# FFN down projections as seven products of half the tokens, half the K and half the columns, with x kept in DRAM

## The chip, the core and the metric

The kernel runs on one core of a Trainium2 chip. The metric is the device time of one execution in microseconds, the median over several executions.

TensorE (PE) multiplies and transposes, VectorE (DVE) and ScalarE (ACT) do elementwise work, GpSimd (POOL) and SyncE (SP) mostly issue DMAs here. ScalarE's queue also issues some DMAs, between its own instructions. Each engine runs its instructions in the order in which the built program lists them, and a waiting instruction holds up all that stand behind it on its engine.

## What is computed

Two layers of a decoder trunk on 512 tokens with D_MODEL 1024. Each layer has a mixer of four parallel branches, and then a SwiGLU feed-forward network (FFN) with residual, which is the part that matters here:

```python
FFN_DIM = ((8 * D_MODEL // 3 + 255) // 256) * 256      # 2816

def hybrid_layer(x, ...):
    ...
    x = x + merged @ w_out

    hf = rmsnorm(x, norm_ffn)
    gate, up = jnp.split(hf @ ffn_w_up, 2, axis=-1)
    return x + (jax.nn.silu(gate) * up) @ ffn_w_down
```

All inputs are float32. The down projection is a product of a 512 x 2816 matrix of activations with the 2816 x 1024 matrix `ffn_w_down[l]`, once for each of the two layers.

## The kernel before

**Three products for one.** Every float32 matrix is kept as a high part in a reduced format (`F32R`) and a low part, the rest. `mm3` (line 267) multiplies two such pairs with three matmuls: high by high, high by low, low by high. In the profile these are lines 270, 271 and 272. A matmul takes a 128x128 stationary tile and up to 512 moving columns.

**Weights.** `Chunk` (line 212) loads one block of weights from DRAM into a `w_raw` tile of 128 x 2048 floats (line 216, on SP's queue), and splits it in pieces of 128 x 1024: ScalarE rounds into `w_hi` (through the helper `A`, line 97), then VectorE subtracts into `w_lo` (line 225). There are two `w_raw` buffers (`RAW_BUFS`) and three each of `w_hi` and `w_lo` (`W_BUFS`). The splits are issued with raised priority (`AHEAD`), and the compiler's scheduler decides where they stand in each engine's order.

**Feature-major and token-major.** `features` has the weights stationary and 512 tokens moving, and its result has features on the partitions. `tokens_wide` has the activations stationary and 512 weight columns moving; its result has tokens on the partitions.

**PSUM.** There are three banks named `mm`, two named `at`, three named `tr` (transposes).

**The FFN** (`ffn`, line 1037) goes through its 2816 inner columns in two parts, of 6 and of 5 chunks of 256 columns. For each chunk it multiplies `h` by the gate and by the up weights (2 x 8 K-tiles x 2 column blocks x 3 = 96 matmuls), scales, applies silu, multiplies, and splits the result into `a_hi` and `a_lo`. After the chunks of a part comes the down projection of that part, with 12 or 10 K-tiles of 128:

- `residual` (line 1000) does it feature-major, for both parts of layer 0 and for the first part of layer 1. For each pair of 128 output columns it loads the weights (1024 KB for 8 K-tiles, then the rest), multiplies, adds the result onto the tile `xT`, which stays in SBUF through the FFN, and in layer 0's second part makes the next layer's `h` (`h_chunk`: cast, difference, square, sum of squares) and sends the chunk of x to the DRAM tensor `x_spill` for the next layer.
- In layer 1's first part, `transposed` turns each finished chunk of `xT` into the token-major `x_tok` with four transposes.
- `final` (line 1023) does layer 1's second part token-major with `tokens_wide`, adds onto `x_tok` and writes the output.

`residual` is also used for the mixer's output projection `w_out`, which reads x from `x_spill` into `xT` (line 987) and makes the FFN's `h`.

Of the kernel before, what the change touches and what calls it, by code (L numbers as in the profile page):

```python
# [69 lines left out]
def hybrid_trunk(ctx: ExitStack, tc: tile.TileContext, x, mem, positions, norm_mix, w_in, conv_w,  # L70
# [41 lines left out]
    def f(ap):  # L112
        return ap.bitcast(F32)
# [153 lines left out]
    def mm3(ps, a, b, first, last):  # L267
        ah, al = a
        bh, bl = b
        pe.matmul(ps, ah, bh, start=first, stop=False)  # L270
        pe.matmul(ps, ah, bl, start=False, stop=False)  # L271
        pe.matmul(ps, al, bh, start=False, stop=last)  # L272

    x_dram = nc.dram_tensor("x_spill", [P, KD, S], F32, kind="Internal").ap()
    kv_dram = [nc.dram_tensor(f"kv{l}", [P, 4, 2, 2, MEM], F32, kind="Internal").ap() for l in range(DEPTH)]
# [225 lines left out]
    def mixer(l, h, norms, cm, cf):  # L501
# [174 lines left out]
        with pool_("dsa") as dp:  # L676
# [46 lines left out]
            with pool_("idx") as ip:  # L723
# [120 lines left out]
                mgp = cf.enter_context(pool_("mgp", "left"))  # L844
# [139 lines left out]
        res = cf.enter_context(tc.tile_pool(name="res", bufs=1))  # L984
# [13 lines left out]
        return h2, ssq2, xT  # L998

    def residual(xT, w2d, a, kt, cols, h2, ssq2, gain, spill=False, done=None):  # L1000
        for m0 in range(0, KD, cols // P):
            ws = []
            k0 = 0
            per = 2048 // cols
            while k0 < kt:
                n = min(per, kt - k0)
                ws.append((k0, n, wchunk(w2d[k0 * P:(k0 + n) * P, m0 * P:m0 * P + cols], n, cols)))
                k0 += n
            pss = [mm_ps() for _ in range(cols // P)]
            for js in ([range(cols // P)] if m0 + cols // P < KD else [[j] for j in range(cols // P)]):  # L1010
                for k0, n, w in ws:
                    features(w, a, js, k0, kt, [pss[j] for j in js])
            for j in range(cols // P):
                m = m0 + j
                dve.tensor_add(xT[:, m, :], xT[:, m, :], pss[j])
                if h2 is not None:
                    h_chunk(h2, ssq2, m, gain(m), xT[:, m, :])
                if spill:
                    nc.scalar.dma_start(x_dram[:, m, :], xT[:, m, :])
                if done is not None:  # L1020
                    done(m)

    def final(x_tok, w2d, a, kt):
        for m0 in range(0, D, 512):
            cols = slice(m0, m0 + 512)
            ws = [wchunk(w2d[k0 * P:min(k0 + 4, kt) * P, cols], min(4, kt - k0), 512) for k0 in range(0, kt, 4)]
            pss = [mm_ps() for _ in range(MM_BUFS)] + [at_ps()]
            tokens_wide(ws, a, kt, pss)
# [87 lines left out]
```

## Time and profile before

| | |
|---|---|
| median of 3 runs | 2047.56 us (2047.41 to 2047.92) |
| the profiled execution | 2047.48 us |
| its span in the profile | 2045.4 us |
| VectorE, ScalarE busy | 62%, 50% of the span |
| granted TensorE clock, mean | 0.999 of full speed |
| moved by DMA | 203.79 MB, 100 GB/s in the mean |
| layer 0: FFN's first up stage, first down stage | from 700 us; 823.6 to 889 us |
| layer 0: second down stage | 1006 to 1060 us |
| layer 1: second down stage | 1987 to 2041 us |

The span runs from the first to the last instruction that the profile shows; the execution's own time is 2 us longer. Rows of a group name line, engine, operation, output and inputs (buffer numbers left out), how often, and times in ns; in the views of one tile they give the shortest, median and longest duration. Rows of waits say who waited for whom, the sum in us, how often and the longest. Rows of DMA issues end with the median time from issue to landing in us.

### The profile page before, as it was taken

What the parts mean: (1) busy time and instruction counts of PE and PEld (TensorE: products, weight loads), DVE (VectorE), ACT (ScalarE), POOL (GpSimd) and SP (SyncE); (2) the same over time, 40 slices, a digit from 0 to 9 for tenths busy, and PEclk for the clock granted to TensorE, in tenths of its full rate; (3) what the DMA queues carried; (4) which work ended last, traced back from release to release, by engine and by line L of the source; (5) the groups of instructions that cost most, each with busy time, mean ns of one, the idle gap of its engine ahead of it and who ended that gap; (6) DMA issues with size and microseconds to landing.
All of it is one profiled execution on the core that took longest, in us unless ns stands there. A gap on an engine that the chain in (4) does not pass through costs nothing.

```text
span 2045.4 us, 26581 instructions
## 1 busy us (share of the span) xinstructions
PE 2034.5 (99%) x10348; PEld 1715.8 (84%) x10348; DVE 1269.3 (62%) x2507; ACT 1017.5 (50%) x1834; POOL 9.8 (0%) x33
## 2 busy tenths in 40 slices
PE   8999999999999999999999999999999999999999
PEld 8998988888888888888889898888888888888887
DVE  6779998547676544334457889963777754533442
ACT  7653655766665423223355456576767633322331
POOL 0000000000000000000000000000000000000000
PEclk9999999999999999999999999999999999999999
DMA  7632232223233232233243213322223322323322
GB/s 253 220 89 94 68 93 93 64 71 93 78 118 113 83 103 93 93 105 102 87 155 94 88 58 107 97 76 63 83 83 101 126 90 96 103 75 111 97 79 93
DMA packets 187709, 203.79 MB, mean 100 GB/s; under 512 B 4270, under 2 KB 176384, under 8 KB 187456
## 3 DMA queue, kind: packets, MB, share of 16 engines
q1 hardware_dynamic: 183872, 193.56, 29.8%
q10 hardware_dynamic: 3552, 8.41, 1.1%
q8 instruction: 81, 1.33, 0.3%
q14 instruction: 44, 0.36, 0.1%
q0 software_dynamic: 160, 0.13, 0.0%
HBM read 191.60 MB, written 10.49 MB: 99 GB/s over the span
## 4 chain that ended last, share of the span: by engine, by line
PE 99%; DMA 1%; DVE 0%; ACT 0%; SPq 0%; issue 0%; DVEq 0%
PE mm L270 30%; PE mm L272 30%; PE mm L271 30%; PE tr L715 1%; PE tr L709 1%; PE at L686 1%; PE at L685 1%; PE at L272 1%; PE at L270 1%; PE at L271 1%; DMA w_raw<-in_mem_w_kv_dram 1%; PE at L963 0%; PE at L937 0%; PE tr L653 0%; PE tr L754 0%; PE tr L972 0%
## 5 line engine op out<-in xcount | busy, mean ns | idle before, releaser
L270 PE MATMUL mm<-h_hi,w_hi 128*128 128x512 f32 x1664 | 653.0, 393 | 0.0
L271 PE MATMUL mm<-h_lo,w_hi 128*128 128x512 f32 x1664 | 652.1, 392 | 0.0
L272 PE MATMUL mm<-h_hi,w_lo 128*128 128x512 f32 x1664 | 650.1, 392 | 0.0
L225 DVE TENSOR_TENSOR w_lo<-w_raw,w_hi 128x1024 fp32r<-128x1024 f32 (+1 forms) x346 | 419.5, 1213 | 364.5 <-ACT w_hi L97 361.3
L97 ACT ACTIVATE w_hi<-w_raw 128x1024 fp32r<-128x1024 f32 (+1 forms) x346 | 363.4, 1051 | 460.8 <-PE mm L271 414.5
L272 PEld LDWEIGHTS mm<-h_hi,w_lo 128*128 128x128 f32 x1664 | 312.8, 188 | 64.8 <-issue 1.2
L270 PEld LDWEIGHTS mm<-h_hi,w_hi 128*128 128x128 f32 x1664 | 312.8, 188 | 64.5 <-issue 2.2
L271 PEld LDWEIGHTS mm<-h_lo,w_hi 128*128 128x128 f32 x1664 | 312.9, 188 | 63.8 <-issue 2.0
L272 PE MATMUL mm<-w_hi,h_lo 128*128 128x256 f32 (+1 forms) x448 | 128.2, 286 | 0.0
L271 PE MATMUL mm<-w_lo,h_hi 128*128 128x256 f32 (+1 forms) x448 | 127.0, 285 | 0.0
L270 PE MATMUL mm<-w_hi,h_hi 128*128 128x256 f32 (+1 forms) x448 | 127.0, 285 | 0.0
L271 PE MATMUL mm<-a_lo,w_hi 128*128 128x512 f32 x272 | 106.3, 391 | 0.0
L270 PE MATMUL mm<-a_hi,w_hi 128*128 128x512 f32 x272 | 106.0, 390 | 0.0
L272 PE MATMUL mm<-a_hi,w_lo 128*128 128x512 f32 x272 | 105.8, 391 | 0.0
L270 PE MATMUL mm<-y_hi,w_hi 128*128 128x512 f32 x256 | 101.4, 397 | 0.0
L272 PE MATMUL mm<-y_hi,w_lo 128*128 128x512 f32 x256 | 100.6, 393 | 0.0
L271 PE MATMUL mm<-y_lo,w_hi 128*128 128x512 f32 x256 | 100.3, 392 | 0.0
L272 PEld LDWEIGHTS mm<-w_hi,h_lo 128*128 128x128 f32 x448 | 85.8, 191 | 1.4 <-issue 0.8
L270 PEld LDWEIGHTS mm<-w_hi,h_hi 128*128 128x128 f32 x448 | 85.3, 191 | 1.2 <-issue 0.8
L271 PEld LDWEIGHTS mm<-w_lo,h_hi 128*128 128x128 f32 x448 | 85.6, 191 | 0.6
L97 ACT ACTIVATE a_hi<-fg 128x512 fp32r<-128x512 f32 x44 | 27.8, 633 | 109.4 <-DVE fg L1065 109.4
L97 ACT ACTIVATE prob<-prob,small 128x128 f32<-128x128 f32 (+3 forms) x128 | 69.2, 554 | 15.2 <-DVE small L698 14.6
(358 smaller groups left out, 2946.9 us busy)
## 6 DMA issues: line engine op xcount, KB each, us to landing
w_raw<-in_w_in_dram SPq DMA_DIRECT2D x72, 1024.0 KB, 5.3
w_raw<-in_ffn_w_up_dram SPq DMA_DIRECT2D x44, 1024.0 KB, 5.1
w_raw<-in_w_lift_dram SPq DMA_DIRECT2D x32, 512.0 KB, 3.5
w_raw<-in_ffn_w_down_dram SPq DMA_DIRECT2D x16, 1024.0 KB, 5.5
w_raw<-in_mem_w_kv_dram SPq DMA_DIRECT2D x8, 1024.0 KB, 5.4
w_raw<-in_w_out_dram SPq DMA_DIRECT2D x8, 1024.0 KB, 5.2
w_raw<-in_ffn_w_down_dram SPq DMA_DIRECT2D x10, 512.0 KB, 3.4
kv<-kv ACTq DMA_DIRECT2D x8, 512.0 KB, 3.2
```

What stands on the lines that cost most here:

```text
L97: i = act.activation(dst, src, func, **kw)
L225: dve.tensor_sub(lo, raw[:, k:e], f(hi))
L270: pe.matmul(ps, ah, bh, start=first, stop=False)
L271: pe.matmul(ps, ah, bl, start=False, stop=False)
L272: pe.matmul(ps, al, bh, start=False, stop=last)
L685: pe.matmul(ps, q[:, hh, s], k[0][:, :n], start=True, stop=False)
L686: pe.matmul(ps, q[:, hh, s], k[1][:, :n], start=False, stop=True)
L709: pe.transpose(pp[:, (2 * e + i) * P:(2 * e + i + 1) * P], probs[2 * i + e][:, b * P:(b + 1) * P], ident)
L715: pe.matmul(pv[e * HD:(e + 1) * HD, :], vt[:, b, :], pt[:, b, e * 2 * P:(e + 1) * 2 * P], start=b == 0, stop=b == t)
```

## The change

The down projection of a part becomes seven products instead of eight, after the scheme of Strassen and Winograd. The activations are cut into two halves of 256 tokens and, in each chunk of 256 inner columns, into two K-tiles of 128 (a "round" is one such pair); the weights into two halves of 512 columns and the same K-tiles. Each of the seven products multiplies a sum or difference of activation blocks with a sum or difference of weight blocks, and the results are collected token-major in a tile `acc`.

- `operands` replaces the split of the activations: it makes the seven activation operands of a round (256 tokens each), high and low.
- `down` replaces `residual` and `final` for the FFN. It runs four passes over the rounds of the part, each with weight loads of its own (`raw_tile` and `split` use the same `w_raw`, `w_hi` and `w_lo` buffers as `Chunk`). Pass one has two products a round with plain weights; pass two two products whose weights are made by two subtractions on VectorE, and one of these differences is written to a new DRAM tensor `t2_spill` by ScalarE's queue; pass three two products, one with a difference; pass four one product, whose weights are a difference with what was written to `t2_spill`. Between the passes `evict` adds the PSUM banks onto `acc`.
- x is no longer held in SBUF through the FFN. The mixer's `residual` writes it to `x_spill`. Layer 1 reads it back in eight chunks during its first part and transposes them into `acc` (`x_in`). Layer 0 adds it at the end: `x_out` reads a chunk on GpSimd's queue into one of three `x_c` buffers, transposes four blocks of `acc`, adds, makes the next `h` and writes the chunk back to `x_spill`. The first four chunks are placed in pass four of the second part, the other four behind it.

```diff
-    def residual(xT, w2d, a, kt, cols, h2, ssq2, gain, spill=False, done=None):
+    def residual(xT, w2d, a, kt, cols, h2, ssq2, gain):
...
+                nc.scalar.dma_start(x_dram[:, m, :], xT[:, m, :])
...
+    def raw_tile():
+        return wpool.tile([P, 2048], F32, name="w_raw", bufs=RAW_BUFS)
+
+    def split(src):
+
+        n = src.shape[1]
+        hi, lo = (wpool.tile([P, 1024], F32R, name=nm, bufs=W_BUFS)[:, :n * 512].rearrange("p (k n) -> p k n", n=512)
+                  for nm in ("w_hi", "w_lo"))
+        with tc.high_priority(offset=AHEAD):
+            A(hi, src, AF.Copy)
+            dve.tensor_sub(lo, src, f(hi))
+        return [(hi[:, k, :], lo[:, k, :]) for k in range(n)]
+
+    def operands(fp, g0, g1):
+
+        hi, lo = (fp.tile([P, 7, HALF], F32R, name=nm, bufs=6) for nm in ("a_hi", "a_lo"))
+
+        def put(o, n, src):
+            h_, l_ = (x[:, o:o + n, :].rearrange("p a b -> p (a b)") for x in (hi, lo))
+            A(h_, src, AF.Copy)
+            dve.tensor_sub(l_, src, f(h_))
+
+        put(A11, 1, g0[:, :HALF])
+        put(A12, 2, g1)
+        dve.tensor_add(g0[:, HALF:], g0[:, HALF:], g1[:, HALF:])
+        dve.tensor_sub(g0[:, :HALF], g0[:, HALF:], g0[:, :HALF])
+        both = g1.rearrange("p (a b) -> p a b", b=HALF)
+        dve.tensor_sub(both, both, g0[:, None, :HALF].to_broadcast([P, 2, HALF]))
+        put(S2, 2, g0)
+        put(S4, 2, g1)
+        return hi, lo
+
+    def down(w2d, ops, spill, evict, between):
+
+        n = len(ops)
+        b0 = mm_ps()
+        ba, bb = [mm_ps(), mm_ps()], [b0, at_ps()]
...
+        def prod(bank, i, o, b, start, stop, more=False):
+            hi, lo = ops[i]
+            for t, ps in enumerate(bank):
+                s = slice(t * P, (t + 1) * P)
+                mm3(ps, (hi[:, o, s], lo[:, o, s]), b, start, stop, more)
+
+        for i0 in range(0, n, 2):
+            m = min(2, n - i0)
+            raw = raw_tile()[:, :m * 1024].rearrange("p (k n) -> p k n", n=512)
+            nc.sync.dma_start(raw, w2d[2 * i0 * P:2 * (i0 + m) * P, C1].rearrange("(k p) n -> p k n", p=P))
+            for i in range(m):
+                p1, p2 = split(raw[:, 2 * i:2 * i + 2, :])
+                prod(ba, i0 + i, A11, p1, i0 + i == 0, i0 + i == n - 1)
+                prod(bb, i0 + i, A12, p2, i0 + i == 0, i0 + i == n - 1)
+        evict(ba, 0, C1, 0)
+        evict(bb, 0, C1, 1)
+        for i in range(n):
+            raw = raw_tile()[:, :1536]
+            nc.sync.dma_start(raw[:, :1024], w2d[2 * i * P:(2 * i + 1) * P, :])
+            nc.sync.dma_start(raw[:, 1024:], w2d[(2 * i + 1) * P:(2 * i + 2) * P, C2])
+            with tc.high_priority(offset=AHEAD):
+                dve.tensor_sub(raw[:, 512:1024], raw[:, :512], raw[:, 512:1024])
+                dve.tensor_sub(raw[:, 1024:], raw[:, 1024:], raw[:, 512:1024])
+            p5, p6 = split(raw[:, 512:].rearrange("p (k n) -> p k n", n=512))
+            nc.scalar.dma_start(spill[:, i, :], raw[:, 1024:])
+            prod(ba, i, S2, p6, False, i == n - 1, True)
+            prod(bb, i, S1, p5, i == 0, i == n - 1)
+        evict(ba, 0, C2, 0)
+        evict(bb, 2, C2, 0)
+        for i0 in range(0, n, 2):
+            m = min(2, n - i0)
+            raw = raw_tile()[:, :m * 1024].rearrange("p (k n) -> p k n", n=512)
+            nc.sync.dma_start(raw, w2d[2 * i0 * P:2 * (i0 + m) * P, C2].rearrange("(k p) n -> p k n", p=P))
+            with tc.high_priority(offset=AHEAD):
+                dve.tensor_sub(raw[:, 0::2, :], raw[:, 1::2, :], raw[:, 0::2, :])
+            for i in range(m):
+                p7, p3 = split(raw[:, 2 * i:2 * i + 2, :])
+                prod(ba, i0 + i, S3, p7, False, i0 + i == n - 1, True)
+                prod(bb, i0 + i, S4, p3, False, i0 + i == n - 1, True)
+        evict(ba, 2, C2, 1)
+        evict(bb, 0, C2, 1)
+        for i0 in range(0, n, 2):
...
+            nc.sync.dma_start(raw[:, :m, :], rows[:, i0:i0 + m, 1, C1])
+            nc.sync.dma_start(raw[:, m:, :], spill[:, i0:i0 + m, :])
+            with tc.high_priority(offset=AHEAD):
+                dve.tensor_sub(raw[:, :m, :], raw[:, :m, :], raw[:, m:, :])
+            for i, p4 in enumerate(split(raw[:, :m, :])):
+                prod(ba, i0 + i, A22, p4, False, i0 + i == n - 1, True)
+            between(i0 // 2)
+        evict(ba, 2, C1, 0)
...
+            def x_chunk(m):
+                xc = fp.tile([P, S], F32, name="x_c", bufs=3)
+                nc.gpsimd.dma_start(xc, x_dram[:, m, :])
+                return xc
...
+            def x_out(m):
+                xc = x_chunk(m)
+                ps = tr_ps()
+                for t in range(NT):
+                    pe.transpose(ps[:, t * P:(t + 1) * P], acc[:, t, m * P:(m + 1) * P], ident)
+                dve.tensor_add(xc, xc, ps)
+                h_chunk(h2, ssq2, m, g_mix(l + 1, m), xc)
+                nc.scalar.dma_start(x_dram[:, m, :], xc)
...
+                    ops.append(operands(fp, *gs))
+                    if fc == 0:
+                        acc = fp.tile([P, NT, D], F32, name="acc")
+                    if last and 0 < fc < 5:
+                        x_in(2 * fc - 2)
+                        x_in(2 * fc - 1)
...
+                def between(i):
+                    if final and not last and i < 2:
+                        x_out(2 * i)
+                        x_out(2 * i + 1)
+
+                down(ffn_w_down[l][f0 * 256:f1 * 256, :], ops, t2_dram[:, l, part], evict, between)
+            if not last:
+                for m in range(4, KD):
+                    x_out(m)
```

`evict` takes the two banks, a token offset, the columns, and whether `acc` already holds a first summand there; it copies (ScalarE, where `acc` holds nothing yet) or adds (VectorE), and in layer 1's second part issues the output DMAs.

115 lines of the change are left out of this document (48 added, 67 removed).

## The prediction

> **What bounds the kernel now.** I read the page's totals first, then TensorE's waits, then one down stage in the view of windows (its columns: busy time of PE, weight load, DVE, ACT and POOL with counts, granted clock, share of the DMA engines, GB/s).
>
> ```profile
> span 2045.4 us, 26581 instructions
> PE 2034.5 (99%) x10348; PEld 1715.8 (84%) x10348; DVE 1269.3 (62%) x2507; ACT 1017.5 (50%) x1834; POOL 9.8 (0%) x33
> ```
>
> ```profile
> PE tr L160 <- DMA rows<-in_mem_k_norm_dram: 1.9, 1, 1.9
> ...
> PE tr L386 <- DVE mt_lo L388: 0.8, 2, 0.6
> ```
>
> ```profile
> 10.00:20.00 10.00, 7.92 (x47) 6.86 (x46) 6.49 (x27) 8.88 (x21) 0.00 (x0) 0.83 1.06 383
> 823.60:889.00 65.40, 65.40 (x290) 54.22 (x289) 21.89 (x23) 13.37 (x13) 0.00 (x0) 1.00 0.30 97
> ```
>
> TensorE sets the time. All its waits are five rows, 6 us in sum, in the first 23 us; after that it never waits for data. The third fence's second row is layer 0's first down stage: 65.4 us, TensorE full, VectorE busy a third, the DMA engines at 30%. It holds 12 K-tiles x 8 column blocks x 3 = 288 products, so one costs 65.4/288 = 0.227 us. The first row there is kept for the clock, below.
>
> A microsecond of matmul taken out is therefore worth a microsecond, as long as the weights still come in time. What prepares them now has room:
>
> ```profile
> SPq L216 <- DVE w_lo L225: 1533.2, 164, 26.6
> ```
>
> Weight loads wait on their queue for 1533 us in sum, 9 us each, for a raw buffer to be released: the split itself waits for TensorE. Everything ahead of TensorE is early, and the two raw buffers suffice because one 1024 KB load feeds 24 products of 512 columns in a down stage (5.4 us).
>
> **The matmuls removed and added.** Three rows of the tile's view give the first products of each down group:
>
> ```profile
> L270 PE MATMUL mm<-a_hi,w_hi x272: 387/390/396, 823.8 to 1875.9; 128*128 128x512 f32 x136
> ...
> L270 PE MATMUL mm<-w_hi,a_hi x60: 388/390/390, 1986.4 to 2038.7; 128*128 128x512 f32 x60
> ...
> L270 PE MATMUL at<-w_hi,a_hi x20: 388/389/390, 1987.7 to 2040.1; 128*128 128x512 f32 x20
> ```
>
> 272 + 60 + 20 = 352 block products, times three is 1056. After the change a pair of K-tiles (a "round") costs 7 products x 2 token tiles x 3 = 42 matmuls instead of 48; there are 11 rounds per layer, so 924 in all. 132 fewer x 0.227 = **-30.0 us**. Layer 1 transposes x 32 times before and after. Layer 0 gets 32 new transposes in `x_out`, at
>
> ```profile
> 35.46 0.44 PE tr L420 x4
> ```
>
> 0.11 us each: **+3.5 us**.
>
> **The extra work of ACT and DVE while the up projections run.** `operands` adds three short subtractions or sums and a larger split to each 256 FFN columns. With the rows of the next fence DVE then has about 13 us and ACT 8 us under 96 matmuls (21.8 us). I price it at nothing; without that cover it would be 3 us for each of the 22 chunks.
>
> **The raw buffers in the second pass.** This is the term that decides. `down` runs four passes. In the second, each round has a raw buffer of its own: 768 KB are loaded, VectorE makes two differences in place, ScalarE and VectorE split two tiles, and ScalarE's queue sends one difference (256 KB) to DRAM from the same buffer. There are still two raw buffers, and the next load into one waits for that spill. The durations:
>
> ```profile
> L225 DVE TENSOR_TENSOR w_lo<-w_raw,w_hi x12: 1224/1225/1226, 1954.8 to 2014.8; 128x1024 fp32r<-128x1024 f32 x12
> L97 ACT ACTIVATE w_hi<-w_raw x11: 1060/1061/1062, 1959.1 to 2013.8; 128x1024 fp32r<-128x1024 f32 x11
> ...
> DMA to landing us min/median/max: 5.0/5.0/5.0
> ```
>
> ```profile
> L1067 DVE TENSOR_TENSOR a_lo<-fg,a_hi x44: 683/693/694, 711.9 to 1990.0; 128x512 fp32r<-128x512 f32 x44
> ```
>
> ```profile
> w_raw<-in_ffn_w_down_dram SPq DMA_DIRECT2D x10, 512.0 KB, 3.4
> ...
> mv<-kv SPq DMA_DIRECT2D x8, 256.0 KB, 3.0
> x_spill<-xT ACTq DMA_DIRECT2D x8, 256.0 KB, 6.1
> ...
> gq_raw<-in_dsa_q_norm_dram POOLq DMA_DIRECT2D x2, 32.0 KB, 4.9
> ```
>
> ```profile
> w_raw<-in_ffn_w_down_dram SPq DMA_DIRECT2D x2, 1024.0 KB, 6.0
> ```
>
> The first fence is the last down stage, whose 512-column loads of 1024 KB land after 5.0 us; the last fence is the window 1006 to 1064, where loads and spills share the engines. A load of 768 KB lies between 3.4 (512 KB) and 5.0: I take 4.3. The spill lies between 2.8, the fastest of its form,
>
> ```profile
> DMA to landing us min/median/max: 2.8/2.8/2.8
> ```
>
> and the median 6.1, when a whole load flows beside it. I take 3.3, nearer the low end, since here a spill meets at most part of one load. One turn of a buffer is 4.3 + 2 x 0.69 + 1.06 + 3.3 + 0.2 for hand-offs = 10.2 us, so the two buffers deliver a round every 5.1 us. TensorE uses a round up in 12 x 0.227 = 2.72 us and waits 2.4. The first two rounds of each part are loaded during the first pass; the other 4 + 3 + 4 + 3 = 14 pay: **+33 us**. By 3.4 and 2.8 the turn is 8.8 and the term 24; by 6.0 and 6.1 it is 14.7 and the term 65. Below the 24 lies only a buffer freed by the split instead of the spill (8.2 us, 19).
>
> The Trainium skill's "DMA: Bandwidth & Descriptors" (Anatomy of one DMA) fits 2.0 us plus bytes at 436 GB/s, for transfers issued by GpSimd. As an estimate from that page the load would take 3.8 us, the spill 2.6, the turn 9.0, and the term would be 25. The trace's 5.0 for 1024 KB is above the page's 4.4, so the rows stand.
>
> **The hand-overs between passes.** Pass three starts with a 1024 KB load into a buffer whose spill has just landed: 5.0 + 1.23 + 1.06 + 1.23 = 8.5 us until its split is done, while the last round on the other buffer ends about 5.1 us after that spill and two matmuls need only the high half: 3.0 us x 4 = 12. In pass four two rounds of one product (2.72 us) use up a load of the same 8.5 us turn, 4.3 per load: two of three loads are 1.5 late, x 8 = 12. The up stage behind the first parts gets its first weights 1 us late, x 2 = 2. **+26 us**, between 14 (the second and third items alone) and 32 (loads of 6.0).
>
> **Queue order.** In the built order VectorE runs three `x_c` sums ahead of a split of layer 0's last pass four, and ScalarE the casts and squares of three `h` chunks ahead of the last split: two late splits, **+2.6 us** (0 to 5). In layer 1 VectorE's difference for the next round stands ahead of this round's `w_lo`, so it waits for that load: 2.5 + 1.0 = **+3.5** (0 to 7).
>
> **The layer boundary.**
>
> ```profile
> L1015 DVE TENSOR_TENSOR xT<-xT,mm x40: 680/687/689, 657.9 to 1876.8; 128x512 f32<-128x512 f32 x40
> ...
> L97 ACT ACTIVATE h_hi<-xT,prm x24: 705/724/726, 658.6 to 1678.0; 128x512 fp32r<-128x512 f32 x24
> L283 DVE SCALAR_TENSOR_TENSOR h_lo<-xT,prm,h_hi x24: 743/746/753, 659.3 to 1679.2; 128x512 fp32r<-128x512 f32 x24
> ```
>
> `x_out` 4 to 7 come after the last product. Each needs an `x_c` buffer that an earlier chunk has spilled (3 us) and GpSimd's queue has refilled (4.9 or more by the page's nearest row, `gq_raw`), then sum, cast, `h_lo` and square sum. The last is ready some 20 us after the last down product; early projections (13.6 us of matmuls) and 12 transposes fill 15 of that. **+5 us** (0 to 15). The end: four sums of 256 columns instead of one behind the last matmul, **+0.8**.
>
> **The clock.** Early in the trace short idle times are followed by slow matmuls:
>
> ```profile
> 12.78 0.51 PE L270 MATMUL mm<-w_hi,mt_hi 128*128 128x256 f32 x2 [1.03 <-ACT w_hi L97]
> 14.04 0.39 PE L271 MATMUL mm<-w_lo,mt_hi 128*128 128x256 f32 x1 [0.76 <-DVE w_lo L225]
> ...
> 14.39 0.28 PE L270 MATMUL mm<-w_hi,mt_hi 128*128 128x256 f32 x1
> 14.51 0.28 PE L271 MATMUL mm<-w_lo,mt_hi 128*128 128x256 f32 x1
> ...
> 16.13 0.41 PE L271 MATMUL mm<-w_lo,mt_hi 128*128 128x256 f32 x1
> 16.34 0.42 PE L272 MATMUL mm<-w_hi,mt_lo 128*128 128x256 f32 x1
> ```
>
> The starts 14.39 and 14.51 are 0.12 us apart, those at 16.13 and 16.34 0.21, and the granted clock between 10 and 20 us was 0.83. So waits of about a microsecond, close together, did cost clock. In the second pass a slow TensorE (5.2 us a round) hides in the 5.1 us turn; it shows at the twelve hand-overs, up to 1.7 us each. I take one in five: **+4** (0 to 20).
>
> **Sum.** -30.0 + 3.5 + 33 + 26 + 2.6 + 3.5 + 5 + 0.8 + 4 = +48 us on the profiled execution's 2047.48 us (span 2045.4 and 2 around it; 0.1 from the median 2047.56): **2096 us**.
>
> **Rivals.**
>
> *TensorE stays the bound.* The split buffers, three deep, and the two raw ones carry it through, and the 30 us come out: 2047.5 - 30 + 3.5 + 1 = 2022 us. It decides if a buffer's turn is at most 5.4 us. For it speaks a DMA share of 0.30; against it that ACT and DVE alone take 2.4 of the turn and the shortest landings of such sizes are 3.4 and 2.8. Chance 5%.
>
> *VectorE sets the pace, the buffers don't.* It has 2 x 0.69 + 1.23 = 2.61 us a round in pass two, as much as TensorE's 2.72, so the two late evictions of a pass (1.4 us) come on top at twelve pass ends: 2022 + 17 = 2039 us. Against it: the same turn. Chance 5%.
>
> *Loads and spills slow each other.* The 6.0 and 6.1 us of the boundary window hold throughout: 65 instead of 33, and 4 more at the hand-overs: 2132 us. Against: here 1 MB of load and spill moves per 5.1 us, 205 GB/s, about half of the 383 GB/s that the window 10 to 20 us shows. Chance 14%.
>
> *The clock drops at every hand-over.* Twelve times 1.7 us instead of 4 in sum: 2112 us. For it the row of 0.83 above; against it that the gaps here, 2.4 us in 5.1, leave TensorE half busy. The Trainium skill's "TensorE: Matmul & The Clock Gate" (Part 1) says that an idle window of about 3.4 us halves the clock and a busy one restores it; by that rule gaps of 2.4 us alone would not do it, whereas the trace's gaps were shorter still. Chance 14%.
>
> **How the numbers follow.** The forecast's own case has 62% and spans 2070 to 2118. The range adds the lower part of the contention case and, below, a turn of 8.8 us with the queue terms at nothing: 2096 - 9 - 14 - 7 = 2066; above, half of the contention: 2128. About 0.2% is what a measurement of this kernel can tell from no change. The two fast rivals give 0.08 for faster, with little near no change (0.02); slower has 0.90.
>
> **What would show it.** TensorE's busy share falls to some 95% or below, and its waits name `w_hi` and `w_lo` in four stretches behind the up stages; the load queue waits for the spill, not for `w_lo`. Inside pass two, starts of rounds lie about 5 us apart, in pass one 2.7. Spills land in 3 to 4 us. The mixers take the same time as before. The forecast is wrong if rounds of pass two start 2.7 us apart, if landings are near 6 us, or if most of the loss lies at the layer boundary.

## The result, and the profile after

The changed kernel takes 2107.76 us in the median of four runs (2106.82 to 2108.65), the kernel before 2047.69 (2047.41 to 2047.92) beside it: a ratio of 1.0293, 95% interval 1.0276 to 1.0311, so 60 us slower. The profiled execution took 2106.82 us.

Page of the changed kernel, its span, the engines' busy times and the chain that ended last:

```profile
span 2105.1 us, 26993 instructions
...
PE 2045.2 (97%) x10248; PEld 1705.5 (81%) x10248; DVE 1429.4 (68%) x2739; ACT 1074.8 (51%) x1918; POOL 18.3 (1%) x49
...
PE 86%; DMA 8%; DVE 4%; ACT 1%; issue 1%; SPq 0%; ACTq 0%; DVEq 0%; POOLq 0%
```

A hundred matmul records fewer, and yet TensorE is busy 11 us longer; DMAs, VectorE and ScalarE now hold 13% of the chain that ends last. Where it happens shows in the windows of the four down stages (from the first to the last matmul with an operand `a_hi` or `a_lo`; the columns are those explained in the prediction, the DMA share and GB/s last):

```profile
824.50:899.20 74.70, 64.41 (x253) 49.36 (x252) 46.32 (x51) 25.72 (x29) 0.00 (x0) 0.93 0.60 196
1009.20:1077.60 68.40, 58.14 (x231) 43.86 (x229) 48.52 (x61) 21.38 (x25) 1.61 (x3) 0.93 0.58 181
1850.70:1925.80 75.10, 64.39 (x254) 48.65 (x253) 50.31 (x58) 23.49 (x24) 0.00 (x0) 0.95 0.61 200
2034.60:2100.80 66.20, 55.05 (x211) 40.27 (x210) 43.57 (x54) 17.98 (x19) 0.00 (x0) 0.95 0.54 183
```

The stages before ran from 823.8, 997.9, 1808.5 and 1986.4 us; layer 0's second is 997.9 to 1052.4 us, not the 1006 to 1060 of the table above. The first had 65.4 us, all of it busy, at a granted clock of 1.00. Now it takes 74.7 with TensorE busy for 64.4, although 252 matmuls at 0.227 us would be 57.2; the clock is 0.93. So each stage has two losses: TensorE stands idle, and what it does it does more slowly. VectorE is busy for 62% of the stage, where it was a third, and is still not full.

The waits say who is late. First TensorE's, then those of the load queue (us in total, times, longest):

```profile
PE mm L270 <- ACT w_hi L97: 31.3, 16, 3.9
PE mm L271 <- DVE w_lo L1027: 7.0, 11, 1.6
PE mm L270 <- DVE acc L1169: 6.8, 6, 3.5
```

```profile
SPq L1074 <- DMA t_spill<-w_raw: 55.9, 14, 5.2
...
SPq L1088 <- DMA t_spill<-w_raw: 41.0, 8, 7.1
```

Line 1074 is pass two's load. Fourteen times it waits for the spill of the difference that the raw buffer still holds, the fourteen rounds that the prediction counted; line 1088, pass three's load, does so eight times. One turn of a buffer stands in the chain of waits of layer 0's first down stage (start us, us, what):

```profile
846.12 0.02 ACT w_hi L97
846.13 5.17 DMA t_spill<-w_raw
...
851.82 5.54 DMA w_raw<-in_ffn_w_down_dram
...
857.46 0.70 DVE w_raw L1078
...
858.32 1.06 ACT w_hi L97
```

The buffer is spilled for 5.2 us, then loaded for 5.5, then differenced and rounded by ScalarE; only after that can TensorE start. The spill leaves as ScalarE's copy begins (846.13 and 846.12), so it runs beside the copy and not behind it. The loads of line 1074, in the view in time of the load queue, follow each other so (the last row is pass three's first load):

```profile
840.15 0.33 SPq L1074 DMA_DIRECT2D w_raw<-in_ffn_w_down_dram  x1
...
845.47 0.33 SPq L1074 DMA_DIRECT2D w_raw<-in_ffn_w_down_dram  x1
...
851.45 0.33 SPq L1074 DMA_DIRECT2D w_raw<-in_ffn_w_down_dram  x1
...
856.69 0.33 SPq L1074 DMA_DIRECT2D w_raw<-in_ffn_w_down_dram  x1
...
861.66 10.69 SPq L1088 DMA_DIRECT2D w_raw<-in_ffn_w_down_dram  x3
```

From 840.15 to 861.66 us a round takes 21.51/4 = 5.4 us where TensorE needs 2.72. What a wait does to the clock shows at the hand-over into pass three (TensorE in time):

```profile
866.24 0.39 PE L272 MATMUL at<-w_hi,a_lo 128*128 128x512 f32 x1
869.62 1.22 PE L270 MATMUL mm<-w_hi,a_hi 128*128 128x512 f32 x2 [2.99 <-ACT w_hi L97]
...
871.90 0.63 PE L271 MATMUL mm<-w_lo,a_hi 128*128 128x512 f32 x1
872.33 0.63 PE L272 MATMUL mm<-w_hi,a_lo 128*128 128x512 f32 x1
...
876.60 0.39 PE L271 MATMUL mm<-w_lo,a_hi 128*128 128x512 f32 x1
876.83 0.39 PE L272 MATMUL mm<-w_hi,a_lo 128*128 128x512 f32 x1
```

After 2.99 us without work the matmuls start 0.43 us apart and are back at 0.23 some 6 us later: this wait costs its own 3 us and about as much again. It is the longest of nine such stretches in the four stages (71 matmuls, shown with some 0.63 us each instead of 0.39); five of them follow a hand-over between passes, four lie inside pass two. The Trainium skill's "TensorE: Matmul & The Clock Gate" (Part 1) gives 426.7 ns from start to start for 512 columns on the throttled array and an idle window of about 3.4 us before it; the spacing agrees, but the gap here was shorter, 2.99 us.

The 59.7 us between the two spans lie in these places (each from the view in time; a down stage from its first to its last product, the boundary from layer 0's last to layer 1's first down product):

| | before | after | difference |
|---|---|---|---|
| four down stages, sum | 242.9 us | 284.5 us | +41.6 |
| layer boundary, with layer 1's mixer and first up stage | 756.1 | 773.1 | +17.0 |
| the two second up stages | 218.2 | 218.7 | +0.5 |
| ahead of the first down stage | 823.8 | 824.5 | +0.7 |

Layer 1's 32 transposes of x have moved to its first up stage, which the boundary contains; before, 26 of them stood in its first down stage (68.3 - 65.4 = 2.9 us) and 6 behind it. Of layer 0's 32 new ones (0.11 us each) 20 stand in the second down stage and 12 behind it. Without transposes the stages lost 41.6 + 2.9 - 2.2 = 42.3 us and the boundary 17.0 - 3.5 - 1.3 = 12.2. Since 132 matmuls are gone, 30 us, the stages lost 72 us against what TensorE's work asks for.

Which pass loses them can be counted. The products run in the order of the passes, 12 for each round in the first three and 6 in pass four; in the first stage passes two, three and four begin at 840.87, 869.62 and 889.32 us. What a pass takes until the next one begins, less 0.227 us a product, is in the four stages together 0.4 us in pass one, 47.7 in pass two, 14.2 in pass three and 12.0 in pass four (2.2 of these are transposes).

### The profile page after: what moved, and what is told of

Read it like the earlier page. It is cut to its first block, busy times and chain, and to the rows that moved or that the text cites. A ratio compares the mean times of both kernels' runs of the same rounds, so it can differ in the third digit from the quotient of the medians.

```text
span 2105.1 us, 26993 instructions
## 1 busy us (share of the span) xinstructions
PE 2045.2 (97%) x10248; PEld 1705.5 (81%) x10248; DVE 1429.4 (68%) x2739; ACT 1074.8 (51%) x1918; POOL 18.3 (1%) x49
## 4 chain that ended last, share of the span: by engine, by line
PE 86%; DMA 8%; DVE 4%; ACT 1%; issue 1%; SPq 0%; ACTq 0%; DVEq 0%; POOLq 0%
PE mm L271 26%; PE mm L270 26%; PE mm L272 26%; DMA w_raw<-in_ffn_w_down_dram 3%; DVE w_lo L1027 1%; DMA t_spill<-w_raw 1%; PE tr L716 1%; ACT w_hi L97 1%; PE tr L710 1%; DMA w_raw<-t_spill 1%; PE at L687 1%; PE at L686 1%; DMA w_raw<-in_w_in_dram 1%; PE at L270 1%; PE at L272 1%
## 5 line engine op out<-in xcount | busy, mean ns | idle before, releaser
L97 ACT ACTIVATE w_hi<-w_raw 128x1024 fp32r<-128x1024 f32 x378 | 397.0, 1053 | 474.7 <-PE mm L271 272.6
L225 DVE TENSOR_TENSOR w_lo<-w_raw,w_hi 128x1024 fp32r<-128x1024 f32 x300 | 365.1, 1218 | 210.8 <-ACT w_hi L97 207.4
L272 PEld LDWEIGHTS mm<-h_hi,w_lo 128*128 128x128 f32 x1664 | 312.9, 188 | 65.5 <-DVE w_lo L225 1.3
L1027 DVE TENSOR_TENSOR w_lo<-w_raw,w_hi 128x1024 fp32r<-128x1024 f32 (+1 forms) x78 | 93.6, 1209 | 57.6 <-ACT w_hi L97 57.3
L270 PE MATMUL mm<-w_hi,a_hi 128*128 128x512 f32 x242 | 83.2, 424 | 34.8 <-ACT w_hi L97 27.9
L97 ACT ACTIVATE a_hi<-fg 128x256 fp32r<-128x256 f32 (+1 forms) x88 | 51.0, 579 | 118.1 <-DVE fg L1150 77.9
L271 PE MATMUL mm<-w_lo,a_hi 128*128 128x512 f32 x242 | 102.0, 422 | 7.6 <-DVE w_lo L1027 7.0
L272 PE MATMUL mm<-w_hi,a_lo 128*128 128x512 f32 x242 | 99.4, 411 | 0.0
L270 PEld LDWEIGHTS mm<-w_hi,a_hi 128*128 128x128 f32 x242 | 46.8, 201 | 53.8 <-ACT w_hi L97 37.9
```

The lines of the kernel that those rows point to most:

```text
L97: i = act.activation(dst, src, func, **kw)
L225: dve.tensor_sub(lo, raw[:, k:e], f(hi))
L270: pe.matmul(ps, ah, bh, start=first, stop=False, skip_group_check=more)
L271: pe.matmul(ps, ah, bl, start=False, stop=False, skip_group_check=more)
L272: pe.matmul(ps, al, bh, start=False, stop=last, skip_group_check=more)
L1027: dve.tensor_sub(lo, src, f(hi))
```

## The experiments

The theory: pass two is paced by the turn of two raw buffers, with the spill as its last leg, and hand-overs follow from it. Against it stand contention on the DMA engines, VectorE's own work, TensorE as the bound, and x through DRAM. Medians are of four runs, ten for the last one. no_diff and seven_plain_weights leave sums of weights out, so they do not compute the product and only their time counts. The stages and the boundary are those of the one profiled execution.

| kernel | us (range) | ratio to before (95%) | four down stages | sum | boundary |
|---|---|---|---|---|---|
| before | 2047.7 | 1 | 65.4, 54.6, 68.3, 54.6 | 242.9 | 756.1 |
| the changed kernel | 2107.8 (2106.8 to 2108.7) | 1.0293 (1.0276 to 1.0311) | 74.7, 68.5, 75.1, 66.2 | 284.5 | 773.1 |
| t2_apart | 2100.7 (2097.4 to 2104.4) | 1.0259 (1.0244 to 1.0274) | 69.6, 59.9, 72.2, 63.3 | 265.0 | 786.2 |
| t2_kept | 2081.0 (2079.5 to 2082.2) | 1.0162 (1.0147 to 1.0177) | 64.3, 58.4, 64.8, 57.2 | 244.7 | 785.9 |
| x_tiles | 2117.3 (2115.0 to 2120.5) | 1.0341 (1.0325 to 1.0356) | 75.0, 69.4, 77.0, 75.1 | 296.5 | 774.2 |
| plain | 2056.7 (2056.6 to 2056.9) | 1.0044 (1.0027 to 1.0061) | 65.4, 56.4, 65.5, 54.6 | 241.9 | 767.7 |
| free_raw | 2070.9 (2069.0 to 2072.0) | 1.0110 (1.0095 to 1.0125) | 62.8, 61.5, 66.0, 58.1 | 248.4 | 770.6 |
| fill | 2121.5 (2119.9 to 2125.7) | 1.0361 (1.0346 to 1.0377) | 73.2, 71.3, 79.7, 70.0 | 294.2 | 777.9 |
| spill_twice | 2127.8 (2123.4 to 2133.8) | 1.0389 (1.0365 to 1.0412) | 81.4, 72.3, 80.7, 70.2 | 304.6 | 774.0 |
| no_diff | 2099.5 (2095.2 to 2100.6) | 1.0249 (1.0233 to 1.0264) | 69.2, 65.0, 77.8, 65.5 | 277.5 | 772.8 |
| kept_x_first | 2074.0 (2073.4 to 2077.7) | 1.0132 (1.0117 to 1.0147) | 66.0, 58.8, 65.2, 57.2 | 247.2 | 776.3 |
| pool_diff | 2073.0 (2067.6 to 2075.0) | 1.0119 (1.0101 to 1.0137) | 63.6, 64.1, 66.5, 57.5 | 251.7 | 767.9 |
| seven_plain_weights | 2046.0 (2044.6 to 2047.1) | 0.9992 (0.9983 to 1.0002) | 59.0, 52.6, 60.6, 51.6 | 223.8 | 774.4 |

The loss by passes, counted as above (us, four stages together, transposes included):

| kernel | pass one | pass two | pass three | pass four |
|---|---|---|---|---|
| the changed kernel | 0.4 | 47.7 | 14.2 | 12.0 |
| t2_apart | 1.8 | 24.7 | 12.4 | 16.0 |
| t2_kept | 1.7 | 13.4 | 12.0 | 7.4 |
| spill_twice | 1.0 | 64.5 | 15.0 | 14.0 |
| no_diff | 4.6 | 32.6 | 11.6 | 18.4 |
| seven_plain_weights | 0.7 | 4.9 | 6.3 | 1.8 |

### The part "token-major, x through DRAM" alone

```diff
-        put(A12, 2, g1)
...
+        for o in range(2):
+            put(2 * o, 1, g0[:, o * HALF:(o + 1) * HALF])
+            put(2 * o + 1, 1, g1[:, o * HALF:(o + 1) * HALF])
...
+        for half, cols in enumerate((C2, C1)):
...
+                    for k, b in enumerate(split(raw[:, 2 * i:2 * i + 2, :])):
+                        for bank, o in ((ba, 0), (bb, 2)):
+                            prod(bank, i0 + i, o + k, b, i0 + i == 0 and k == 0, i0 + i == n - 1 and k == 1)
```

> Edit: the seven products are replaced by the eight plain ones, token-major, with the same tiles, x through DRAM, and the same layer boundary: 1056 matmuls in the down stages as in the kernel before, no sums of weights or activations, no spill. It does the part 'token-major, x through DRAM' alone. Theory (the loss sits in pass two's buffer turn and its hand-overs): the kernel before's 2047.7, +3.5 for layer 0's 32 transposes, +5 to +12 for the boundary, 2060 us (2054 to 2066). Rival (most of the loss comes from x through DRAM, the token-major evictions and the boundary): above 2080.

Measured 2056.7 us, within the range. In the windows of its first and third stage TensorE has no gap and its full clock:

```profile
824.00:889.00 65.00, 65.00 (x289) 53.81 (x288) 16.68 (x16) 17.16 (x21) 0.00 (x0) 1.00 0.28 96
...
1822.00:1887.30 65.30, 65.30 (x289) 54.07 (x289) 21.41 (x24) 13.46 (x14) 0.00 (x0) 1.00 0.30 97
```

So the layout and x through DRAM cost 9 us. The boundary is 767.7 - 756.1 = 11.6 us longer, the down stages and the up stages between them 2 us shorter. Of the 11.6 us 5.1 are transposes (layer 1's 32, and 14 of the new ones), and 6.5 the longer way to the next layer's `h`. The other 51 us come with the seven products.

### The spill out of the buffer, and no spill

t2_apart gives the second difference a tile of its own; t2_kept keeps it there until pass four.

```diff
-                dve.tensor_sub(raw[:, 1024:], raw[:, 1024:], raw[:, 512:1024])
-            p5, p6 = split(raw[:, 512:].rearrange("p (k n) -> p k n", n=512))
-            nc.scalar.dma_start(spill[:, i, :], raw[:, 1024:])
+                dve.tensor_sub(t2, raw[:, 1024:], raw[:, 512:1024])
+            p5, p6 = split2(raw[:, 512:1024], t2)
+            nc.scalar.dma_start(spill[:, i, :], t2)
```

In t2_kept the last line is `t2s.append(t2)`, and pass four subtracts `t2s[i0 + i]` without loading anything from the spill.

> Edit: pass two writes its second difference into a 2 KB tile of its own (the up stage's g and u tiles, idle then), and splits and spills it from there; same arithmetic, same bytes, 22 more copies on ScalarE and 22 more subtractions on VectorE, each of half the width. Theory (the turn of the two raw buffers sets pass two, and the spill is its last leg): the raw buffer comes free after load 5.1, two differences 0.69 each, and the copy and subtraction of half a tile, about 0.6 each, so about 7.9 us for a turn, 3.9 us a round where it was 5.1. Over the 14 paying rounds that is -17, with some of the hand-overs after them: 2085 us (2075 to 2093). Rival one (loads and spills slow each other on the DMA engines): the bytes are the same, so 2103 to 2110. Rival two (VectorE's and ScalarE's work sets the pace): 2107 to 2115.

> Edit: as t2_apart, but the second differences stay in those six tiles until pass four, which subtracts them from there; no spill and no loads of it. Theory of the turn: pass two as in t2_apart, pass four's loads half as long: 2080 us (2070 to 2090), little below t2_apart. Rival one (contention of spills and loads): nearly the whole gain comes here and none in t2_apart, 2060 to 2080 against 2107. Rival two (work of VectorE and ScalarE): 2105 to 2115.

t2_apart came out at 2100.7, 8 us above the range given for the theory and 2 us under that of the contention rival. The median alone would have decided for neither. The stages decide: with the same bytes they are 19.5 us shorter (284.5 to 265.0), and in the first stage the loads of pass two now follow each other by 3.4, 2.3, 3.6, 3.6 and 3.3 us. What hides it is the boundary, 13 us longer. ScalarE there, in time:

```profile
1072.59 0.61 ACT L97 ACTIVATE sq<-x_c 128x512 f32<-128x512 f32 x1
1078.91 1.06 ACT L97 ACTIVATE w_hi<-w_raw 128x1024 fp32r<-128x1024 f32 x1 [5.71 <-PE mm L271]
...
1079.87 0.71 ACT L97 ACTIVATE h_hi<-x_c,prm 128x512 fp32r<-128x512 f32 x1
```

The scheduler has put a split of the next `w_in` ahead of two chunks of `h`. That split waits 5.7 us for TensorE to release a `w_hi`, and the chunks that TensorE is short of stand behind it.

t2_kept came out at 2081.0, where the theory put it, but with a larger step from t2_apart than the theory allowed: its stages are another 20.3 us shorter. By passes 11 of these lie in pass two, where only the writes are missing, and 9 in pass four, where the loads of the spill are. The writes do slow loads that run beside them: of pass two's first loads of a round (512 KB) the five to seven whose landing is on record land after 4.2 to 5.3 us in t2_apart and 3.5 to 3.9 in t2_kept. In the changed kernel five are on record, with 3.6 to 4.1; the pair of loads in the chain above took 5.5 us beside the other buffer's spill. So of the 72 us the spill is worth 40: 23 in pass two as a leg of the turn, 11 there by its writes, and most of the rest in pass four. The contention rival, which expected nearly the whole gain in this step, is wrong as the only cause and right about part of it.

### The spill doubled, the differences left out

```diff
             nc.scalar.dma_start(spill[:, i, :], raw[:, 1024:])
+            nc.scalar.dma_start(other[:, i, :], raw[:, 1024:])
```

> Edit: the changed kernel with each second difference written to DRAM twice, the second time into a buffer of its own that nothing reads: 22 more writes of 256 KB on ScalarE's queue, from the same raw buffer. Theory (the spill is the last leg of the raw buffer's turn): the second write ends 1 to 3 us after the first, half of that in each of the 14 paying rounds and as much again at the hand-overs: 2107.8 + 7 to 28, 2124 us (2115 to 2138). Rival (the spill counts only as traffic: 5.8 MB on top of 247 MB): 2106 to 2112.

```diff
-                dve.tensor_sub(raw[:, 512:1024], raw[:, :512], raw[:, 512:1024])
-                dve.tensor_sub(raw[:, 1024:], raw[:, 1024:], raw[:, 512:1024])
```

> Edit: the changed kernel without the two subtractions of weights in pass two (the sums B2 - B1 and the one from it are left out, so that the products take the plain weights); loads, splits and spills as they are. Theory (the raw buffer's turn, each leg of it counts): the turn is 2 x 0.69 shorter, half of that a round, 14 x 0.69 = 10 us, and a few us at the hand-overs: 2107.8 - 10 to 18, 2095 us (2088 to 2100). Rival (the DMA engines' traffic sets the round, and the differences run beside it): 2105 to 2110.

Two writes instead of one make the kernel 20.0 us slower (2127.8, within the range), all of it in the stages (+20.1), and 17 of it in pass two. The writes land later too (the view of DMA issues, median us to landing, for the changed kernel and for spill_twice):

```profile
t_spill<-w_raw ACTq DMA_DIRECT2D x22, 256.0 KB, 3.9
```

```profile
t_spill<-w_raw ACTq DMA_DIRECT2D x44, 256.0 KB, 4.6
```

Without the differences it is 8.3 us faster (2099.5), at the slow end of the range; three stages are shorter by 0.7 to 5.5 us, layer 1's first is 2.7 longer. By passes it gains 15 us in pass two, within the 10 to 18 that the theory asked for, and loses 4 in pass one and 6 in pass four; why these are later stays open. So both the spill and the differences count as legs of the turn, and their sizes are known to some us only.

### More work for TensorE

```diff
+            if i:
+                fill(i, 4)
             prod(ba, i, S2, p6, False, i == n - 1, True)
...
+                if i0 + i == 0:
+                    fill(0, 8)
```

The last two lines stand in passes three and four. That makes 18 x 4 + 8 x 8 = 136 matmuls, 31 us (the expectation counted 144).

> Edit: the changed kernel with 144 further matmuls of 128x512 in the down stages, into a PSUM tile that nothing reads, ahead of most rounds of pass two and of the first rounds of passes three and four: 144 x 0.227 = 33 us more work for TensorE. Theory (TensorE waits for buffers there, and what it loses besides is the lower clock after those waits): the work fits into the 46 us of waits for the most part, and the granted clock of the four down stages rises from 0.93 to 0.95 towards 1: 2098 us (2090 to 2110). Rival one (TensorE is the bound): 2107.8 + 33 = 2141. Rival two (the waits cover the work but the clock stays where it is): 2108 to 2118.

It costs 13.7 us (2121.5), between the ranges of the two rivals: more than half of the 31 us lay in waits, and TensorE is not the bound. The gain from the clock that the theory expected did not come. The windows of the first stage and of layer 1's first stage:

```profile
824.00:897.00 73.00, 67.74 (x289) 54.88 (x288) 47.09 (x52) 26.57 (x30) 0.00 (x0) 0.98 0.59 202
...
1855.00:1935.00 80.00, 71.57 (x292) 56.69 (x290) 50.70 (x58) 23.81 (x24) 0.00 (x0) 0.94 0.56 189
```

The clock rose from 0.93 to 0.98 in the one and the stage got 1.5 us shorter; in the other it did not (0.95 to 0.94), and the stage got 4.6 us longer. In layer 0's second stage it rose from 0.93 to 0.95, in layer 1's second it stayed at 0.95; both got longer. How much of the loss is the clock's own is not settled by this.

### The boundary

```diff
-                xc = fp.tile([P, S], F32, name="x_c", bufs=3)
+                if not last and m >= 3:
+                    xc = fp.tile([P, S], F32, name="fg" if m < 7 else "fu", bufs=4 if m < 7 else 2)
+                else:
+                    xc = fp.tile([P, S], F32, name="x_c", bufs=3)
```

> Edit: at layer 0's end the chunks 3 to 7 of x are read into the up stage's idle g and u tiles, not into the ring of three x_c tiles, so that no read waits for an earlier chunk's write to DRAM. Nothing else is changed. Theory: the boundary lost about 12 us against the kernel before, and the wait for three tiles is most of it: 2098 us (2094 to 2102). Rival (the boundary is lost to the late weights of the next stage and to the lower TensorE clock after the hand-over): 2106 to 2109.

A miss (2117.3, above both ranges): the boundary is 774.2 us, 1.1 longer, although no read waits for a tile and the last sum of x comes at 1092.3 us, not at 1094.3. So the ring of three tiles was not the loss. That the whole kernel is 9.5 us slower comes from elsewhere: the built order of layer 1's second down stage changed with it, and TensorE's waits there for `w_lo` grew from 3.1 to 9.6 us, its clock fell from 0.95 to 0.89.

```diff
-                ps = tr_ps()
...
+                with tc.high_priority(offset=2 * AHEAD):
+                    ps = tr_ps()
...
```

> Edit: t2_kept with a higher priority for layer 0's x_out (its transposes, the sum, the h chunk and the write of x), so that ScalarE and VectorE are given x's chunks ahead of the splits of w_in that would wait for TensorE; nothing else. Theory (in t2_apart and t2_kept the boundary is 13 us longer than in the changed kernel because ScalarE's order has a split of w_in, which waits for a free w_hi, ahead of the chunks of x that TensorE waits for): from layer 0's last down product to layer 1's first 785.9 us become 770 to 774, the time 2081 - 13 = 2068 us (2064 to 2072). Rival (the longer boundary comes from the x_c tiles or from the DMAs of x): 2077 to 2083.

The boundary of t2_kept went from 785.9 to 776.3 us, the time from 2081.0 to 2074.0: order alone gives back 9.6 of the 13 us. The time lies between the two ranges, 2 us above the theory's, and the view shows a cause for the rest: ScalarE still waits 4.2 us at one split with a chunk of `h` behind it:

```profile
1074.27 1.06 ACT L97 ACTIVATE w_hi<-w_raw 128x1024 fp32r<-128x1024 f32 x1 [4.19 <-PE mm L271]
...
1075.23 0.71 ACT L97 ACTIVATE h_hi<-x_c,prm 128x512 fp32r<-128x512 f32 x1
```

### The buffer free after the differences, and then GpSimd

free_raw is t2_kept with pass two's first difference, too, in a tile of its own, and x read into other tiles at the boundary. pool_diff moves the second difference to GpSimd.

```diff
-                dve.tensor_sub(raw[:, 512:1024], raw[:, :512], raw[:, 512:1024])
...
+                dve.tensor_sub(d5, raw[:, :512], raw[:, 512:1024])
+                dve.tensor_sub(t2, raw[:, 1024:], d5)
+            p5, p6 = split2(d5, t2)
```

> Edit: as t2_kept, and pass two's first difference goes into a tile of the x_c ring, so that the raw buffer is free after the two differences; x_c gets a fourth tile, and at layer 0's end chunks 4 to 7 of x are read into the idle g tiles. Theory: the turn falls to load 5.1 + 2 x 0.69 + 0.2, 6.7 us or 3.3 us a round; what t2_kept still waited at the hand-over into pass three (2.0 to 2.9 us in each of four stages) shrinks, and the boundary, which took 13 us more in t2_kept than in the changed kernel (1059.3 to 1843.4 us against 1080.6 to 1850.7), goes back to about its length, since ScalarE's order there is that of the changed kernel again: 2081 - 13 - 6 = 2062 us (2054 to 2072). Rival (the rate of the loads, not the buffers, sets pass two and the hand-over): stages as in t2_kept, 2068 to 2081 by the boundary alone.

> Edit: free_raw with pass two's second difference on GpSimd instead of VectorE. In free_raw VectorE runs pass two nearly without a gap (four operations of 0.6 to 0.7 us a round beside the evictions). Theory (VectorE is what is next once the buffers are free): 22 operations of 0.69 less on it, 15 us, of which the hand-overs get a part: 2071 - 4 to 10, 2064 us (2058 to 2069). Rival (GpSimd's subtraction is so much slower, or holds up VectorE so much, that the second weight of each round comes later): 2072 to 2090.

free_raw ran in 2070.9 us, within the theory's range, but as the rival described it: the boundary fell by 15.3 us, the stages not at all (244.7 to 248.4; layer 0's second overlaps the boundary more here). So freeing the raw buffer still earlier is worth nothing in the stages. VectorE is nearly full now, and still waits for loads; in layer 0's second down stage, in time:

```profile
1017.05 0.68 DVE L1090 TENSOR_TENSOR fg<-w_raw,x_c 128x512 f32<-128x512 f32 x1
1017.66 0.68 DVE L1036 TENSOR_TENSOR w_lo<-x_c,w_hi 128x512 fp32r<-128x512 f32 x1
1018.26 0.68 DVE L1089 TENSOR_TENSOR x_c<-w_raw 128x512 f32<-128x512 f32 x1
1018.86 0.68 DVE L1036 TENSOR_TENSOR w_lo<-fg,w_hi 128x512 fp32r<-128x512 f32 x1
...
1022.87 0.69 DVE L1089 TENSOR_TENSOR x_c<-w_raw 128x512 f32<-128x512 f32 x1 [2.12 <-DMA w_raw<-in_ffn_w_down_dram]
```

For some 9 us it runs without a gap, 2.4 us a round, with the evictions between; then it waits 2.12 us for a load. Which of the two sets the pace is not settled. GpSimd did not relieve VectorE: 2073.0 us, where the rival put it, and with ranges that overlap no difference to free_raw. In pool_diff, GpSimd's group and two of VectorE's subtractions beside it, then one with nothing beside it:

```profile
L1090 POOL TENSOR_TENSOR fg<-w_raw,x_c 128x512 f32<-128x512 f32 x16 | 23.8, 1489 | 809.6 <-DVE x_c L1089 646.1 <-DMA w_raw<-in_ffn_w_down_dram 161.8 <-ACT w_hi L97 1.6
```

```profile
2020.86 1.28 DVE L1036 TENSOR_TENSOR w_lo<-x_c,w_hi 128x512 fp32r<-128x512 f32 x1 [0.78 <-ACT w_hi L97]
...
2023.86 1.53 DVE L1036 TENSOR_TENSOR w_lo<-fg,w_hi 128x512 fp32r<-128x512 f32 x1
...
2026.51 0.68 DVE L1036 TENSOR_TENSOR w_lo<-x_c,w_hi 128x512 fp32r<-128x512 f32 x1
```

### Seven products without sums of weights

```diff
-            with tc.high_priority(offset=AHEAD):
-                dve.tensor_sub(raw[:, 0::2, :], raw[:, 1::2, :], raw[:, 0::2, :])
...
-            nc.sync.dma_start(raw[:, m:, :], spill[:, i0:i0 + m, :])
```

Pass two here loads two rounds at a time, as pass three does, and takes the plain blocks.

> Edit: the changed kernel's seven products with plain weights: each pass loads the blocks two rounds at a time as pass one does, splits them and multiplies; all sums of weights, the spill and its loads are left out, the sums of activations, the passes, the evictions and x through DRAM stay. Theory (TensorE's gain of 132 matmuls is there, and what it costs to supply the summed weights has taken it): the kernel 'plain' less 132 x 0.227 = 30 us, 2056.7 - 30 = 2027 us (2024 to 2034), the down stages near 57.3, 49.4, 57.3 and 47.8 us. Rival one (the passes themselves cost, by accumulation over two passes with an eviction between, and by the sums of activations in the up stages): 2035 to 2060. Rival two (each weight is used for half as many matmuls, so loads, copies and splits set the pace even without sums): 2060 or more.

Measured 2046.0 us: rival one, and the most telling run. With no sum of weights at all, the seven products only draw level with the kernel before. The stages are 223.8 us, where 241.9 - 30.0 = 211.9 would be TensorE's work. The largest of TensorE's waits names the reason (us in total, times, longest):

```profile
PE mm L270 <- DVE acc L1161: 6.5, 7, 1.4
```

At the end of each pass banks are added onto `acc` and used again in the next, and TensorE waits for the sum; plain has two such ends in a stage, the seven products four. These waits are 6.5 of the 12 us; another 2.3 are waits for split weights, and the remaining 3 are not named. Against plain the gain is 18.1 us in the stages, and 6.7 of it goes again at the boundary (774.4 against 767.7).

## Why the prediction was right

The forecast was 2096 us with 2066 to 2128; 2107.8 lies in the range, 12 us from the value, with the mechanism that was named first. About 7 of the 12 us are the boundary and 3 the stages. By its steps:

- **132 matmuls fewer, -30; 32 transposes, +3.5.** The work is as priced. That it could be collected was not examined: seven_plain_weights gets 18 of the 30 in the stages.
- **Operands beside the up projections, 0.** Right: the two second up stages are 0.5 us longer together, 1.2 without the transposes that left them.
- **Two raw buffers in pass two, +33, and hand-overs, +26; with queue order 2.6 and 3.5 and the clock 4, 69 us in the stages.** Measured 72. By place: pass two with the hand-over behind it was to lose 33 + 12 + 3.5 = 48.5 us and lost 47.7; pass four 12 + 2.6 and lost 10 without its transposes; pass three nothing but a share of the clock's 4, and lost 14.2. A term was missing there: TensorE's waits for the sums on `acc`, which are 6.8 us over all hand-overs (the row above).
- **The turn.** Forecast 10.2 us, 5.1 a round. Over the 14 rounds a load follows the one before it in the same buffer by 8.1 to 13.1 us, 10.1 in the mean (starts of line 1074's loads). Its legs are not those of the forecast, so that it fits to 0.1 us is luck. ScalarE's copy, 1.06 us, was a leg and is none, since the spill runs beside it. From the load's issue to the spill's it took 6.15 us in the mean, where 4.3 + 1.38 was priced, and from there to the next load 3.95, where the spill was priced at 3.3. That the turn sets pass two does not rest on these sizes: doubling the spill, taking it out of the turn and taking the differences out moved the stages by +20.1, -19.5 and -7.0 us, each in the direction that the turn asks for.
- **Waits and clock.** The waits were to be 65 us and the clock 4. TensorE's gaps in the four windows are 284.4 - 242.0 = 42.4 us, and its busy time is 242.0, where 924 x 0.227 and 20 transposes are 212: 30 us more. The granted clock, 0.05 to 0.07 short over these windows, accounts for about 17 of them; the others are not named. Of the nine slow stretches four (29 matmuls) lie inside pass two, where the prediction let the turn hide a slow TensorE. Five follow hand-overs, with 42 matmuls at 0.43 instead of 0.23 us: 8 us, where one hand-over in five was taken, 4 us. Slow matmuls count as busy; that is part of why TensorE's busy share fell only to 97%, where 95% or less was to show.
- **The layer boundary, +5.** Mis-sized: 12.2. plain shows 6.5 for x through DRAM by itself; the rest comes only with the seven products, beside late weights and a clock of 0.91 in the 29 us behind the last product (0.94 in plain), and no run separates these. The reason given, the ring of three tiles, is refuted by x_tiles.
- **The tail, +0.8.** From the last product to the end of the span it is 4.3 us, as long as before.
- **The rivals.** TensorE as the bound is out by fill. VectorE as the pace is out by t2_apart, where it had no less work (1431.1 us busy against 1429.4) and the stages were shorter. Contention had 14% as an alternative; by t2_apart and t2_kept it is a part, inside the terms that the forecast took from the turn. The clock at every hand-over, also 14%, priced 2112 us, nearer to the measured time than the forecast; its mechanism is out, since seven of the twelve hand-overs have no slow matmuls behind them.
- **Two slips in its working.** A load of 1024 KB fed 48 products before, not 24 (288 products in a stage use 6 MB), so the kernel before had twice the room that it states; no term hangs on this. And the range's lower end takes off 9, 14 and 7 us, where its own bounds give 33 - 24 = 9, 26 - 14 = 12 and 2.6 + 3.5 = 6.1, so 2069.

No version ran faster than the kernel before beyond what the measurement tells. The best with seven products that computes the whole down projection is free_raw (pool_diff and kept_x_first are within 3.1 us), 37 us faster than the changed kernel and 23 slower than the one before.

## What to carry to other kernels

Fewer matmuls are worth their time only if each operand still feeds as many of them: here 1024 KB of loaded weights fed 48 matmuls before, 24 in passes one and three, and in pass two 768 KB feed 12, and differences and a spill were added to a buffer that had two copies. Work out the turn of the scarcest buffer, leg by leg up to the last reader, a spill included, and compare it with the time that the consumer needs per turn. And look at the gain without its price: the seven products with no sum of weights lost 12 of their 30 us in the stages, 7 at the boundary and 9 to the layout that they need, and were level with the kernel before.

## What was not expected of the hardware

- Behind waits TensorE ran stretches of 6 to 14 matmuls at about half speed, and the length of the last wait does not tell when. 2.99 us was followed by matmuls 0.43 us apart until 875.7 us, and in no_diff 1.97 us (before 854.46) by the same until 858.4; in t2_kept 2.89 us (before 859.89) was followed by matmuls 0.23 us apart. What decides is not shown by these runs.
- A GpSimd subtraction of two 128x512 float tiles took 1.49 us against 0.68 on VectorE, and VectorE's own lasted 1.28 and 1.53 us where they ran beside it. The Trainium skill's "GPSIMD Engine Reference" (Specifications; Engine selection) says that the two share their SBUF interface and that GpSimd is about twice as slow with two inputs; the trace agrees.
